# Attention iterations in another fixed order, with squares of q and k moved to POOL

## The chip, the cores and the metric

The kernel runs on one core of one Trainium2 chip. The core has five engines with a queue of instructions each: TensorE (PE: matmuls, and transposes that are done as matmuls with an identity), VectorE (DVE), ScalarE (ACT), GpSimd (POOL) and SyncE (SP), which issues most DMAs. An engine runs its queue in order; it waits for another engine through semaphores. Matmuls read SBUF and write PSUM; DVE and ACT read PSUM, POOL does not. The metric is the device time of one execution in microseconds (us).

## What is computed

Two encoder layers over 256 positions of 1024 features, in float32. Each layer has an attention half and an FFN half:

```python
h = rmsnorm(x, attn_norm[l])
c_q, c_kv, k_r, q_d, k_d, v_d = jnp.split(h @ w_in[l], split_at, axis=-1)
o_a = mla_mixer(c_q, c_kv, k_r, cos, sin, ...)          # 8 heads of 96, dense softmax over 256 keys
q_d = rmsnorm(q_d.reshape(B, S, DIL_HEADS, DIL_HD), g_dil_q[l])
k_d = rmsnorm(k_d.reshape(B, S, DIL_HEADS, DIL_HD), g_dil_k[l])
o_b = dilated_attention(q_d, k_d, v_d, rel_bias)        # 8 heads of 64, three patterns with bias
mixed = jnp.concatenate([o_a.reshape(B, S, -1), o_b.reshape(B, S, -1)], axis=-1)
x = x + mixed @ w_out[l]
x = x + conv_ffn(rmsnorm(x, ffn_norm[l]), w_up[l], conv_w[l], conv_b[l], w_down[l])
```

The norms of q_d and k_d need a sum of squares over the 64 features of each head. The three dilated patterns are folded into one additive matrix `Bn`, so a dilated head is a softmax over all 256 keys too.

## The kernel before

**Products in two parts.** Each float32 product is done as three faster matmuls: an operand is split into a high part and a low part, and hi x hi, lo x hi and hi x lo are summed in PSUM. The high part of a weight (`wh`) is a copy on ACT (L175), the low part (`wl`) is raw minus `wh` on DVE (L188); the same is done for activations (`xh` and `xl`, `mh` and `ml`). Weights stream in from DRAM by SP's DMAs, in units of 128x1024, and a ring of six units holds `wh` and `wl`. `W.fill()` splits the next unit when the ring has room; the low part lags by one unit, `LO_LAG`.

**One layer.** After the in-projections come nine iterations, n = 0 to 8. Iteration n computes the scores of head pair n (four MLA pairs, four dilated pairs, and nothing at n = 8), and finishes pair n - 1: it turns the probabilities p (transposes on PE, `turn_p`, L591), copies them from PSUM on ACT, multiplies by v (`values`, L600) and keeps the result as mh and ml (`keep_o`). `turn_qk` (L528) transposes q and k of the next pair into PSUM, and `keep_qk` copies k on ACT and q, with its gain, on DVE (L279). `maxima` and `normalise` run on DVE, `exponents` on ACT. The dilated maxima also add the bias (L566). The transposes of p, q and k use one PSUM buffer, tile name A: a new turn waits until the last one has been copied out. The scores use S, and the values O.

**Filling work.** In between, at `gemm()`, PE does steps from the list `steps`: what is left of the k projection, the v projection and the output projection (tile acc; six or three matmuls of 512 columns a step). `COUNTS` says how many steps an iteration takes, and they are spread evenly over four slots. The end of the output projection (`ou[5]`, `ou[6]` and `out_end`, which adds to x), the transposition and split of x (`xT_part`: turn on L431, gain on DVE, square and xh on ACT, xl on DVE) and the first blocks of the FFN (`up`, L1083 to L1085, with half of the input rows) follow.

**Dilated q and k.** `d_evac` copies a 128x512 tile of q or k from PSUM to `nat` on ACT, and squares it on ACT from PSUM; `d_sum` adds up the squares on DVE into `ssd`; `d_var` (POOL), one DVE round and a chain of small POOL operations make an inverse root (`rsqrt` in `d_factor`) for all heads, and `d_scale` multiplies the two `nat` tiles by it on POOL (L290). The dilated turns read these tiles.

**What sets the order.** The nine iterations stand in a `manual_schedule` for PE, DVE and ACT: the order of the code is the order of these queues. POOL's queue, and everything behind the iterations, is ordered by the scheduler.

Of the kernel before, what the change touches and what calls it, by code (L numbers as in the profile page):

```python
# [19 lines left out]
P = 128  # L20
# [27 lines left out]
START = 5  # L48
COUNTS = [3, 4, 4, 4, 4, 4, 5, 4, 3]
WARM = 8  # L50
# [86 lines left out]
class Weights:  # L137
# [60 lines left out]
    def fill(self, most=1):  # L198
        limit = min(len(self.units), self.n_done + W_BUFS - W_SLACK)
        for _ in range(most):  # L200
            if self.n_hi < limit:
                self.split_hi()
            if self.n_lo < self.n_hi - LO_LAG:
                self.split_lo()

    def get(self, u):
# [25 lines left out]
def encoder(ctx: ExitStack, tc: tile.TileContext, wpk, x, prm, cst, oh, rb, pos, out):  # L232
# [53 lines left out]
    def act(o, a, f, **kw):  # L286
        nc.scalar.activation(o, a, f, **kw)  # L287
# [220 lines left out]
    def run(steps):  # L508
        for s in steps:
            s()  # L510
# [100 lines left out]
    def layer(l, sx, late, bias):  # L611
# [26 lines left out]
        def d_evac(i, dst, t, a):  # L638
            act(dst[:, t, :], a, AF.Copy)
            sq = wide()  # L640
            act(sq, a, AF.Square)
            return sq
# [30 lines left out]
        def v_evac(t):  # L673
            act(vd[:, t, :], a_v[t], AF.Copy, scale=sx.r[:, t:t + 1])
# [241 lines left out]
        run(gk[:START - 3])  # L916
        hm = Heads(l, True, qm, km, vbox[0], pairs, fq)
        hm.turn_qk(0)
        hm.keep_qk(0)
# [53 lines left out]
        def iteration(n):  # L973
# [5 lines left out]
            turns = list(nxt[0].turns(nxt[1])) if nxt else []  # L979
            slots = 4 if nxt or cur else 2  # L980
            share = [len(todo) // slots + (i < len(todo) % slots) for i in range(slots)]

# [13 lines left out]
            def background():  # L996
                if side:
                    side.pop(0)()

            if n == 3:  # L1000
                v_evac(0)
                v_evac(1)
            if cur:
                cur[0].scores(cur[1])
                cur[0].maxima(cur[1])
            if prev:
                prev[0].turn_p(prev[1])
            if cur:
                cur[0].maxima(cur[1] + 1)
                cur[0].exponents(cur[1])  # L1010
            W.fill()
            gemm()
            if prev:
                prev[0].turn_p(prev[1] + 1)
            if cur:
                cur[0].exponents(cur[1] + 1)
            background()
            gemm()
            if prev:
                prev[0].values(prev[1])  # L1020
                prev[0].keep_o(prev[1])
            background()
            turn_next()
            if cur:
                cur[0].normalise(cur[1])
            W.fill()
            background()
            gemm()
            turn_next()
            if cur:  # L1030
                cur[0].normalise(cur[1] + 1)
            background()
            gemm()
            W.fill()
            while side:
                background()
            assert not todo

        with tc.manual_schedule(engines={mybir.EngineType.PE, mybir.EngineType.DVE, mybir.EngineType.Activation}):
            for n in range(HEADS + 1):  # L1040
                iteration(n)
        run(steps)
        run(ou[5][2:3])
        W.fill()

        def out_end(t, c):
            out_mm(7, t, c, final=True)
            xs = X[:, t, 512 * c:512 * c + 512]
            tt(xs, accs[t][c], xs, ALU.add)

        run(ou[5][3:])
        out_end(0, 0)
        out_end(1, 0)
        run(ou[6][2:])
        xT_part(sf, gf, 0, 0)
        xT_part(sf, gf, 1, 0)
        out_end(0, 1)
        out_end(1, 1)
        W.done(u_out[7])
        W.fill()  # L1060

# [75 lines left out]
        first = [[acc(), acc()], [bank(), bank()]]  # L1137
        for j in range(2):
            up(j, first[j], range(4))
            W.fill()  # L1140
        xT_part(sf, gf, 0, 1, tbank())
        xT_part(sf, gf, 1, 1, obank())
        for j in range(NF):
# [114 lines left out]
```

## Time and profile before

| | us |
|---|---|
| median of three runs | 660.03 (659.01 to 660.3) |
| the profiled execution | 659.02 |
| its span | 657.2 |
| PE busy | 636.5 (97%) |
| DVE busy | 493.7 (75%) |
| ACT busy | 399.6 (61%) |
| POOL busy | 67.5 (10%) |

The profiled execution took 1.8 us more than its span, and lies at the low end of the three runs. Busy shares are means over the whole execution; the places where PE waits are short, and are found in the lists of waits and in the timelines. A duration in a timeline is that of the instruction by itself; consecutive instructions of an engine overlap at their ends, so what an instruction costs in a row is the distance between starts.

### The profile page before, as it was taken

To read this page: it belongs to the slowest core of one execution; us is meant where nothing else is said; L and a number is where in the kernel's file an instruction comes from. 1 tells how busy PE (TensorE), PEld (TensorE's weight loads), DVE (VectorE), ACT (ScalarE), POOL (GpSimd) and SP (SyncE) were. 2 spreads that over 40 slices of the span, in tenths; PEclk is the share of its full clock that TensorE was granted. 3 is DMA by queue.
4 is the path that set the end of the run, shared out by engine and by line. 5 is a ranking of instruction groups with operands and counts; after the bars stand their busy time and mean duration, and the time that the engine had idled before them with its cause. 6 is when DMAs were issued, how large, how long until landed. Compare 5 with 4: busy or idle time off the path is not lost.

```text
span 657.2 us, 10655 instructions
## 1 busy us (share of the span) xinstructions
PE 636.5 (97%) x4018; PEld 554.3 (84%) x4018; DVE 493.7 (75%) x1006; ACT 399.6 (61%) x721; POOL 67.5 (10%) x177
## 2 busy tenths in 40 slices
PE   8989899989999999999999989999899999999997
PEld 7867676679999999999899876667899999999996
DVE  5796676677987777778699766667699777777773
ACT  6972976756755555555478467766385555555551
POOL 3850170000000000000001105400000000000000
PEclk9999999999999999999999999999899999999999
DMA  8759431252664555554347422313247545544401
GB/s 300 269 194 173 179 128 65 65 192 79 237 207 183 192 193 192 192 177 154 112 136 272 161 78 115 128 65 129 65 168 280 181 175 175 184 189 188 161 1 64
DMA packets 17708, 105.19 MB, mean 160 GB/s; under 512 B 2103, under 2 KB 3800, under 8 KB 6649
## 3 DMA queue, kind: packets, MB, share of 16 engines
q1 hardware_dynamic: 17656, 104.51, 45.9%
q8 instruction: 31, 0.51, 0.3%
q14 instruction: 21, 0.16, 0.1%
HBM read 103.20 MB, written 1.31 MB: 159 GB/s over the span
## 4 chain that ended last, share of the span: by engine, by line
PE 83%; POOL 6%; DVE 5%; ACT 2%; issue 2%; DMA 1%; SPq 1%; DVEq 0%; ACTq 0%; POOLq 0%
PE S L1085 12%; PE S L1084 12%; PE S L1083 12%; PE acc L1129 6%; PE acc L1128 6%; PE acc L1127 6%; PE acc L492 3%; PE acc L491 3%; PE acc L490 3%; PE O L600 3%; POOL s L295 3%; PE S L551 2%; PE A L591 2%; PE acc L935 2%; PE acc L938 2%; PE acc L937 2%
## 5 line engine op out<-in xcount | busy, mean ns | idle before, releaser
L175 ACT ACTIVATE wh<-raw 128x1024 fp32r<-128x1024 f32 (+3 forms) x188 | 193.2, 1036 | 110.6 <-PE S L1084 64.8
L188 DVE TENSOR_TENSOR wl<-raw,wh 128x1024 fp32r<-128x1024 f32 (+3 forms) x188 | 223.6, 1192 | 28.7 <-ACT wh L175 28.1
L1084 PE MATMUL S<-xl,wh 128*128 128x256 f32 x640 | 181.3, 284 | 0.0
L1085 PE MATMUL S<-xh,wl 128*128 128x256 f32 x640 | 180.9, 283 | 0.0
L1083 PE MATMUL S<-xh,wh 128*128 128x256 f32 x640 | 180.3, 283 | 0.0
L1084 PEld LDWEIGHTS S<-xl,wh 128*128 128x128 f32 x640 | 122.7, 192 | 1.5
L1083 PEld LDWEIGHTS S<-xh,wh 128*128 128x128 f32 x640 | 122.4, 192 | 1.6
L1085 PEld LDWEIGHTS S<-xh,wl 128*128 128x128 f32 x640 | 122.7, 192 | 0.1
L284 DVE SCALAR_TENSOR_TENSOR t<-t,prm_s,t 128x255 f32<-128x255 f32 x176 | 74.0, 480 | 1.0 <-ACT t L287 0.9
L1129 PE MATMUL acc<-wl,mh 128*128 128x512 f32 x176 | 69.3, 394 | 0.0
L1127 PE MATMUL acc<-wh,mh 128*128 128x512 f32 x176 | 69.3, 394 | 0.0
L1128 PE MATMUL acc<-wh,ml 128*128 128x512 f32 x176 | 69.2, 393 | 0.0
L490 PE MATMUL acc<-wh,xh 128*128 128x512 f32 (+2 forms) x160 | 61.3, 383 | 0.9 <-ACT nat L287 0.9
L492 PE MATMUL acc<-wl,xh 128*128 128x512 f32 (+2 forms) x160 | 58.2, 364 | 0.4 <-DVE wl L188 0.4
L491 PE MATMUL acc<-wh,xl 128*128 128x512 f32 (+2 forms) x160 | 57.8, 361 | 0.0
L287 ACT ACTIVATE t<-A 128x512 f32<-128x512 f32 (+2 forms) x56 | 28.1, 503 | 45.3 <-PE A L528 23.3
L287 ACT ACTIVATE t<-t,prm_s 128x256 f32<-128x256 f32 x88 | 47.9, 593 | 4.7 <-DVE t L275 4.7
L287 ACT ACTIVATE mh<-t 128x256 fp32r<-128x256 f32 x44 | 18.3, 416 | 47.7 <-DVE t L275 47.7
L275 DVE TENSOR_TENSOR t<-S,r2b 128x512 f32<-128x512 f32 (+1 forms) x42 | 28.0, 666 | 24.0 <-PE S L1085 24.0
L1129 PEld LDWEIGHTS acc<-wl,mh 128*128 128x128 f32 x176 | 33.1, 188 | 7.5
L1127 PEld LDWEIGHTS acc<-wh,mh 128*128 128x128 f32 x176 | 33.4, 190 | 5.9
L1128 PEld LDWEIGHTS acc<-wh,ml 128*128 128x128 f32 x176 | 33.1, 188 | 6.1
(168 smaller groups left out, 974.2 us busy)
## 6 DMA issues: line engine op xcount, KB each, us to landing
raw<-in_wpk_dram SPq DMA_DIRECT2D x86, 1024.0 KB, 4.8
raw<-in_wpk_dram SPq DMA_DIRECT2D x3, 896.0 KB, 4.6
raw<-in_wpk_dram SPq DMA_DIRECT2D x3, 768.0 KB, 4.9
raw<-in_wpk_dram SPq DMA_DIRECT2D x2, 816.0 KB, 5.9
Bn<-scr SPq DMA_DIRECT2D x8, 192.0 KB, 11.3
raw<-in_wpk_dram SPq DMA_DIRECT2D x2, 720.0 KB, 5.6
X<-in_x_dram SPq DMA_DIRECT2D x4, 256.0 KB, 5.3
raw<-in_wpk_dram SPq DMA_DIRECT2D x2, 384.0 KB, 5.6
```

Source lines behind the costliest of these rows:

```text
L175: self.nc.scalar.activation(hi[:, :n], self.raw[t][:, o:o + n], AF.Copy, scale=1.0 if g is None else g)
L188: self.nc.vector.tensor_tensor(out=lo[:, :n], in0=raw, in1=hi, op=ALU.subtract)
L287: nc.scalar.activation(o, a, f, **kw)
L490: mm(o, lhs.hi[:, k, sl], rh, start=k == 0, stop=False)
L491: mm(o, lhs.lo[:, k, sl], rh, start=False, stop=False)
L492: mm(o, lhs.hi[:, k, sl], rl, start=False, stop=k == ktot - 1)
L1083: mm(o, hi[:, kp], sf.hi[:, k, :], start=k == 0, stop=False)
L1084: mm(o, hi[:, kp], sf.lo[:, k, :], start=False, stop=False)
L1085: mm(o, lo[:, kp], sf.hi[:, k, :], start=False, stop=k == 7)
L1127: mm(o, m.hi[:, 0, sl], hi[:, cs], start=j == 0, stop=False)
L1128: mm(o, m.lo[:, 0, sl], hi[:, cs], start=False, stop=False)
L1129: mm(o, m.hi[:, 0, sl], lo[:, cs], start=False, stop=j == NF - 1)
```

## The change

Five things are changed.

- `COUNTS` and the new table `SHARES` give each iteration five slots for the filling steps, in place of four equal ones. The last iterations have 5 and 2 steps, where they had 4 and 3.
- The iteration is written in another order: both maxima first, a slot, `turn_p` of the first head, and `turn_next` ahead of the values. `W.fill` is divided into `fill_hi`, which stands twice in an iteration, and `fill_lo`, which stands two or three times and has no lag. `normalise` of the first head is ahead of the values, that of the second behind the first `fill_lo`. `v_evac` moves from the start of iteration 3 to the end of iteration 2.
- The manual order also covers the end of the output projection and the first two `up` blocks. `xT_part` is written out as `gained` (turn, gain, xh), `low` (xl) and `xT_square`, and the squares stand last.
- The squares of dilated q and k are computed on POOL from the copy in SBUF, four of 128x512 per layer.
- A one-column Exp stands ahead of the first `turn_qk`.

```diff
-COUNTS = [3, 4, 4, 4, 4, 4, 5, 4, 3]
+COUNTS = [3, 4, 4, 4, 4, 4, 5, 5, 2]
+SHARES = {(3, False, 2): (0, 0, 1, 1, 1), (4, True, 2): (0, 1, 1, 1, 1), (4, True, 1): (1, 1, 2, 0, 0),
+          (5, True, 1): (1, 1, 2, 1, 0), (5, True, 0): (1, 2, 2, 0, 0), (2, True, 0): (0, 1, 1, 0, 0)}
...
+    def fill_hi(self):
+        if self.n_hi < min(len(self.units), self.n_done + W_BUFS - W_SLACK):
+            self.split_hi()
+
+    def fill_lo(self):
+        if self.n_lo < self.n_hi:
+            self.split_lo()
...
             act(dst[:, t, :], a, AF.Copy)
             sq = wide()
-            act(sq, a, AF.Square)
+            ptt(sq, dst[:, t, :], dst[:, t, :], ALU.mult)
...
+        act(small(2)[:, :1], ones[:, :1], AF.Exp)
         hm.turn_qk(0)
...
-            slots = 4 if nxt or cur else 2
-            share = [len(todo) // slots + (i < len(todo) % slots) for i in range(slots)]
+            share = SHARES[len(todo), bool(prev), len(turns)]
+            share = list(share)
...
             if cur:
                 cur[0].scores(cur[1])
                 cur[0].maxima(cur[1])
+                cur[0].maxima(cur[1] + 1)
+            gemm()
+            if not side:
+                W.fill_lo()
+            background()
             if prev:
                 prev[0].turn_p(prev[1])
+            else:
+                turn_next()
             if cur:
-                cur[0].maxima(cur[1] + 1)
                 cur[0].exponents(cur[1])
-            W.fill()
             gemm()
             if prev:
                 prev[0].turn_p(prev[1] + 1)
             if cur:
                 cur[0].exponents(cur[1] + 1)
-            background()
             gemm()
+            if prev:
+                turn_next()
+            if cur:
+                cur[0].normalise(cur[1])
             if prev:
                 prev[0].values(prev[1])
                 prev[0].keep_o(prev[1])
-            background()
-            turn_next()
-            if cur:
-                cur[0].normalise(cur[1])
-            W.fill()
+            W.fill_hi()
+            W.fill_lo()
             background()
             gemm()
             turn_next()
             if cur:
                 cur[0].normalise(cur[1] + 1)
             background()
+            W.fill_hi()
+            background()
             gemm()
-            W.fill()
-            while side:
-                background()
+            W.fill_lo()
+            if n == 2:
+                v_evac(0)
+                v_evac(1)
...
+            out_end(0, 0)
+            out_end(1, 0)
+            run(ou[6][2:3])
+            pv0 = gained(0, 0, xT_turn(0, 0))
+            run(ou[6][3:])
+            pv1 = gained(1, 0, xT_turn(1, 0))
+            W.fill_hi()
+            low(0, 0, pv0)
+            low(1, 0, pv1)
+            W.fill_lo()
+            out_end(0, 1)
+            out_end(1, 1)
+            W.done(u_out[7])
+            xT_square(sf, 0, 0)
+            W.fill_hi()
+            W.fill_lo()
+            xT_square(sf, 1, 0)
```

Three places show what this does to the queues. The lines of the changed kernel have higher numbers for the same code (L290 becomes L300, L295 L305, L188 L190, L279 L289, L275 L285, L582 L592, L566 L576).

**POOL, layer 0, up to the start of the chain for dilated q.** `ssd` holds the sums of squares, `s` are small tiles of the chain, `nat_171` is q and `nat_172` is k. Before:

```order
L295 TENSOR_SCALAR s_739<-s_738 128x16 [waits Pool_49]
L295 TENSOR_SCALAR s_1053<-e_77_409 128x2 [waits DVE_49,Activation_49]
L295 TENSOR_SCALAR s_1052<-ssd_173,s_1053 128x8 [waits DVE_49,Pool_49]
L295 TENSOR_SCALAR s_1052<-ssd_173,s_1053 128x8 [waits DVE_49]
L290 TENSOR_TENSOR s_1061<-s_1058 128x16 [waits DVE_49]
L295 TENSOR_SCALAR s_1064<-s_1061 128x16 [waits Pool_49]
```

and in the changed kernel:

```order
L305 TENSOR_SCALAR s_739<-s_738 128x16 [waits Pool_49]
L300 TENSOR_TENSOR t_198_968<-nat_171 128x512 [waits Activation_49]
L300 TENSOR_TENSOR t_199_973<-nat_171 128x512 [waits Activation_49]
L305 TENSOR_SCALAR s_1064<-e_77_409 128x2 [waits DVE_49]
L305 TENSOR_SCALAR s_1063<-ssd_173,s_1064 128x8 [waits DVE_49,Pool_49]
L300 TENSOR_TENSOR t_245_1123<-nat_172 128x512 [waits Activation_49]
L305 TENSOR_SCALAR s_1063<-ssd_173,s_1064 128x8 [waits DVE_49]
L300 TENSOR_TENSOR s_1072<-s_1069 128x16 [waits DVE_49]
L305 TENSOR_SCALAR s_1075<-s_1072 128x16 [waits Pool_49]
L300 TENSOR_TENSOR s_1073<-s_1075,s_1063 128x16 [waits Pool_49]
L305 TENSOR_SCALAR s_1079<-s_1073 128x16 [waits Pool_49]
L300 TENSOR_TENSOR s_1078<-s_1079,s_1069 128x16 [waits Pool_49]
```

The two squares of q stand ahead of the chain, the first square of k stands between the two `d_var` of q; the second follows right behind the last row shown, inside the chain.

**DVE, layer 0, from the end of iteration 3 to the first dilated maxima.** The row L279 or L289 on A is `keep_qk`, the rows on t are `normalise`. Before:

```order
L275 TENSOR_TENSOR ml_1346<-O_1340,mh_1345 128x256 [waits Activation_49]
L279 TENSOR_SCALAR t_311_1354<-A_1349,gqk 128x256 [waits Activation_49]
L582 RECIPROCAL s_1358<-s_1302 128x2
L279 TENSOR_SCALAR t_291_1300<-t_291_1300,s_1358 128x256 [waits DVE_49]
L279 TENSOR_SCALAR t_291_1300<-t_291_1300,s_1358 128x256
L582 RECIPROCAL s_1365<-s_1315 128x2
L279 TENSOR_SCALAR t_297_1313<-t_297_1313,s_1365 128x256 [waits DVE_49]
L279 TENSOR_SCALAR t_297_1313<-t_297_1313,s_1365 128x256
L188 TENSOR_TENSOR wl_1374<-raw_923,wh_1288 128x1024
```

and in the changed kernel:

```order
L289 TENSOR_SCALAR t_309_1347<-A_1342,gqk 128x256 [waits Activation_49]
L592 RECIPROCAL s_1351<-s_1294 128x2
L289 TENSOR_SCALAR t_292_1292<-t_292_1292,s_1351 128x256 [waits DVE_49]
L289 TENSOR_SCALAR t_292_1292<-t_292_1292,s_1351 128x256
L285 TENSOR_TENSOR ml_1361<-O_1355,mh_1360 128x256 [waits Activation_49]
L190 TENSOR_TENSOR wl_1366<-raw_946,wh_1364 128x1024 [waits DMAHW2_49,Activation_49]
L592 RECIPROCAL s_1368<-s_1300 128x2
L289 TENSOR_SCALAR t_296_1298<-t_296_1298,s_1368 128x256 [waits DVE_49]
L289 TENSOR_SCALAR t_296_1298<-t_296_1298,s_1368 128x256
L190 TENSOR_TENSOR wl_1374<-raw_946,wh_1372 128x1024 [waits Activation_49]
L576 ISA t_318_1384,s_1385<-S_1378,Bn 128x256 [waits DMAHW5_49,DMAHW4_49,DMAHW6_49,DMAHW3_49,DMAHW7_49,DMAHW0_49,PE_49]
```

One weight split without a wait, ahead of the maxima, has become two, each waiting for ACT, with the second head's `normalise` between them. Iteration 4 ends in the same way, iterations 5 to 7 with one split.

**DVE, layer 0, iteration 8.** `t_377` and `t_382` (before), `t_378` and `t_381` (after) are p of the last two heads, which PE turns next. Before:

```order
L275 TENSOR_TENSOR ml_1657<-O_1651,mh_1656 128x256 [waits Activation_49]
L582 RECIPROCAL s_1660<-s_1619 128x2
L279 TENSOR_SCALAR t_377_1617<-t_377_1617,s_1660 128x256 [waits DVE_49]
L279 TENSOR_SCALAR t_377_1617<-t_377_1617,s_1660 128x256
L582 RECIPROCAL s_1667<-s_1631 128x2
L279 TENSOR_SCALAR t_382_1629<-t_382_1629,s_1667 128x256 [waits DVE_49]
L279 TENSOR_SCALAR t_382_1629<-t_382_1629,s_1667 128x256
L188 TENSOR_TENSOR wl_1676<-raw_1109,wh_1607 128x1024
```

and in the changed kernel:

```order
L592 RECIPROCAL s_1666<-s_1625 128x2 [waits Activation_49]
L289 TENSOR_SCALAR t_378_1623<-t_378_1623,s_1666 128x256 [waits DVE_49]
L289 TENSOR_SCALAR t_378_1623<-t_378_1623,s_1666 128x256
L285 TENSOR_TENSOR ml_1676<-O_1670,mh_1675 128x256 [waits Activation_49]
L190 TENSOR_TENSOR wl_1681<-raw_1313,wh_1679 128x1024 [waits DMAHW5_49,Activation_49]
L592 RECIPROCAL s_1683<-s_1630 128x2
L289 TENSOR_SCALAR t_381_1628<-t_381_1628,s_1683 128x256 [waits DVE_49]
L289 TENSOR_SCALAR t_381_1628<-t_381_1628,s_1683 128x256
```

The first head's `normalise` has moved ahead of ml, the second head's behind a weight split that waits for ACT.

## Rows read from the trace of the kernel before

**Rows 1.** The page: busy us, share and instructions of PE and PEld.

```profile
PE 636.5 (97%) x4018; PEld 554.3 (84%) x4018; DVE 493.7 (75%) x1006; ACT 399.6 (61%) x721; POOL 67.5 (10%) x177
```

**Rows 2.** A time window: busy us by engine, granted clock, DMA share, GB/s.

```profile
100.00:120.00 20.00, 20.00 (x112) 13.11 (x111) 14.04 (x51) 13.07 (x34) 0.00 (x0) 1.00 0.21 60
```

**Rows 3.** PE's waits, 62 to 165 us: total us, times, longest.

```profile
PE A L528 <- DVE t L279: 2.5, 3, 1.0
PE acc L1083 <- ACT xh L287: 2.1, 1, 2.1
PE S L551 <- DVE t L279: 0.7, 1, 0.7
```

**Rows 4.** The same view, 380 to 475 us (layer 1).

```profile
PE A L528 <- POOL nat L290: 0.2, 1, 0.2
```

**Rows 5.** Timeline of POOL: start, us, operation, idle before and releaser.

```profile
83.14 1.29 POOL L290 TENSOR_TENSOR s<-s,s 128x16 f32<-128x16 f32 x1
...
86.58 2.05 POOL L290 TENSOR_TENSOR nat<-nat,fd 128x512 f32<-128x512 f32 x2
...
90.30 0.28 POOL L295 TENSOR_SCALAR s<-ssd,e 128x8 f32<-128x8 f32 x1 [1.29 <-DVE ssd L645]
91.08 0.21 POOL L290 TENSOR_TENSOR s<-s 128x16 f32<-128x16 f32 x1 [0.50 <-DVE s L281]
...
97.73 2.04 POOL L290 TENSOR_TENSOR nat<-nat,fd 128x512 f32<-128x512 f32 x2
```

**Rows 6.** Timeline of PE, first dilated iteration.

```profile
101.48 1.13 PE L551 MATMUL S<-t,t 64*128 64x256 f32 x8
...
105.17 1.66 PE L600 MATMUL O<-t,nat 128*64 128x256 f32 x8
106.76 0.66 PE L528 MATMUL A<-cst_s,nat 128*128 128x128 f32 x4
107.17 0.47 PE L935 MATMUL acc<-wh,mh 128*128 128x512 f32 x1
...
108.73 1.14 PE L551 MATMUL S<-t,t 64*128 64x256 f32 x8
```

**Rows 7.** Timeline of DVE beside the stretched POOL operation.

```profile
83.12 1.22 DVE L188 TENSOR_TENSOR wl<-raw,wh 128x1024 fp32r<-128x1024 f32 x1
```

**Rows 8.** Timeline of DVE, first dilated iteration.

```profile
101.74 0.16 DVE L582 RECIPROCAL s<-s 128x2 f32<-128x2 f32 x1
...
102.46 1.22 DVE L188 TENSOR_TENSOR wl<-raw,wh 128x1024 fp32r<-128x1024 f32 x1
103.59 0.42 DVE L566 CUSTOM_DVE_ANT_0 t<-S,Bn 128x256 f32<-128x256 f32 x1
...
107.28 0.42 DVE L275 TENSOR_TENSOR ml<-O,mh 128x256 fp32r<-128x256 f32 x1 [2.23 <-ACT mh L287]
```

**Rows 9.** Timeline of ACT, the same stretch.

```profile
100.19 0.39 ACT L287 ACTIVATE t<-A 128x256 f32<-128x256 f32 x1 [0.56 <-PE A L528]
100.47 1.05 ACT L175 ACTIVATE wh<-raw 128x1024 fp32r<-128x1024 f32 x1
...
104.11 0.51 ACT L287 ACTIVATE t<-t,s 128x256 f32<-128x256 f32 x1 [0.28 <-DVE s L566]
...
105.12 0.57 ACT L287 ACTIVATE t<-A 128x512 f32<-128x512 f32 x1
...
106.86 0.39 ACT L287 ACTIVATE mh<-O 128x256 fp32r<-128x256 f32 x1 [0.18 <-PE O L600]
```

**Rows 10.** Timelines of DVE, ACT and PE at the first FFN matmul, layer 0.

```profile
141.42 0.69 DVE L275 TENSOR_TENSOR t<-S,prm_s 128x512 f32<-128x512 f32 x1
...
142.25 0.62 ACT L287 ACTIVATE xh<-t 128x512 fp32r<-128x512 f32 x1
...
142.92 0.50 PE L1083 MATMUL acc<-xh,wh 128*128 128x256 f32 x2 [2.06 <-ACT xh L287]
```

**Rows 11.** A time window in layer 1, columns as in rows 2.

```profile
462.90:466.30 3.40, 3.40 (x18) 3.40 (x17) 2.62 (x4) 1.25 (x3) 0.49 (x2) 0.51 0.40 169
```

More of the change, by code (lines that the diff above doesn't have):

```diff
@@ L1032, in iteration @@
             background()
+            W.fill_hi()
+            background()
             gemm()
[L1034 to L1036 removed]
+            W.fill_lo()
+            if n == 2:
+                v_evac(0)
+                v_evac(1)
+            assert not side
             assert not todo
@@ L1041, in layer, with out_end, gained, low @@
                 iteration(n)
[L1042 to L1060, printed above, removed]
+            run(steps)
+            run(ou[5][2:])
+            W.fill_hi()
+            W.fill_lo()
+            def out_end(t, c):
+                out_mm(7, t, c, final=True)
+                xs = X[:, t, 512 * c:512 * c + 512]
+                tt(xs, accs[t][c], xs, ALU.add)
+            def gained(t, c, pt):
+                tv = wide()
+                pv = tv.rearrange("p (k t) -> p k t", k=4)
+                tt(pv, pt.rearrange("p (k t) -> p k t", k=4),
+                   gf[:, 4 * c:4 * c + 4].unsqueeze(2).to_broadcast([P, 4, P]), ALU.mult)
+                act(sf.hi[:, 4 * c:4 * c + 4, t * P:t * P + P], pv, AF.Copy)
+                return pv
+            def low(t, c, pv):
+                sl = slice(t * P, t * P + P)
+                tt(sf.lo[:, 4 * c:4 * c + 4, sl], pv, sf.hi.bitcast(F32)[:, 4 * c:4 * c + 4, sl], ALU.subtract)
+            out_end(0, 0)
[12 more added lines that the diff above has]
+            xT_square(sf, 0, 0)
+            W.fill_hi()
+            W.fill_lo()
+            xT_square(sf, 1, 0)
         r2b = work.tile([P, SEQ], F32, name=nm("r2b"), tag="r2b", bufs=1)
@@ L1137, in layer @@
         first = [[acc(), acc()], [bank(), bank()]]
[L1138 to L1142, printed above, removed]
+        with tc.manual_schedule(engines={mybir.EngineType.PE, mybir.EngineType.DVE, mybir.EngineType.Activation}):
+            up(0, first[0], range(4))
+            W.fill_hi()
+            W.fill_lo()
+            pv2 = gained(0, 1, xT_turn(0, 1, tbank()))
+            up(1, first[1], range(4))
+            pv3 = gained(1, 1, xT_turn(1, 1, obank()))
+            low(0, 1, pv2)
+            low(1, 1, pv3)
+            xT_square(sf, 0, 1)
+            xT_square(sf, 1, 1)
         for j in range(NF):
```

3 lines of the change are left out of this document (removed).

## The prediction

> **What bounds the kernel now.** I read the page first: TensorE (PE) is busy 97% of the span [rows 1], so an edit can only pay where PE waits, or cost where it makes PE wait. The time windows say where it does not wait: between 100 and 120 us, in the dilated iterations, PE is busy 20.00 of 20 us [rows 2], so nothing is to be won there. The list of waits names the places that are left. In layer 0, PE waits 2.5 us in three pieces for DVE before turns of q and k (L528), 0.7 us for DVE before scores (L551), and 2.1 us for ACT's xh before the first FFN matmul (L1083) [rows 3]; each piece also costs about 0.16 us of a drained pipeline (the distance between the starts of the matmuls on both sides is that much more than the wait). That is 3.3 + 2.2 = 5.5 us, with drains near 6, in layer 0; layer 1 repeats it. One more row matters most: in layer 1 PE waits 0.2 us for POOL's scaled `nat` at L528 [rows 4]. The wait is small only because PE arrives late. The chain on POOL that scales k for the dilated heads ends at 97.73 + 2.04 = 99.77 us in layer 0 [rows 5], and PE turns that tile right behind it. So two chains run neck and neck up to the first dilated scores at 101.48 [rows 6], and removing PE's waits shortens one of them.
>
> **The change, part by part.** Sums are per layer, against the profiled execution: 659.0 us, of which 657.2 span. That run lies 1.0 below the median of the three.
>
> *First half (iterations 0 to 3).* Both maxima move ahead of the filling matmuls, the turns of q and k move earlier in DVE's and ACT's order, normalise comes earlier, and the dummy Exp loads the table while ACT waits for something else in the k chain. I followed each old wait of [rows 3] through the new order: the producer (keep_qk on DVE) no longer stands behind maxima or a weight split, and the three L528 pieces and the L551 piece vanish or shrink. That would bring PE to the turn of dilated pair 0 some 3.3 to 4 us earlier. But there it needs the POOL chain, and the change makes that longer. The square of k, t = 0, stands between the two `d_var` of q, and that of k, t = 1, inside the factor chain of q. A 128x512 operation on POOL takes 2.04 / 2 = 1.02 us [rows 5]. The q chain ended at 86.58 + 2.05 = 88.63; now at about 89.6 with one square inside, 90.6 if the other is late too. Then two `d_var` at about 0.3 each and the round over DVE, 90.30 to 91.08, then 91.08 to 99.77 [rows 5]: 89.6 + 0.3 + 0.3 + 0.5 + 8.7 = 99.4, against 99.77. Before, POOL stood idle ahead of 90.30 waiting for DVE's sum; that idle time is what pays for the square. The chain also holds two operations stretched to 1.29 us, 1.08 more than their neighbours, exactly while DVE splits a weight (83.14 against 83.12 [rows 5, 7]; four such pairs a layer). If both in the k chain fell elsewhere the chain would be 2.2 shorter; if both squares come late it is about 1.1 longer. Net: **-0.6 us** (-2.2 to +1.1), and PE now waits some 3 us in one piece where it waited in four.
>
> The Trainium skill (SBUF — State Buffer, section "SBUF: two separate sides") says that DVE and GpSimd hold a shared port pair exclusively for a whole instruction, when a DVE operation has two SBUF inputs and GpSimd reads SBUF; the other blocks. The trace agrees in one direction, the 1.29 beside the 1.22. By that rule a square would hold a weight split for up to 1.02 us, which no row shows; it is a rival below.
>
> *Dilated iterations 4 and 5.* Here the new order puts two weight splits on DVE at the tail of iterations 3 and 4 (before: one), each waiting for its copy on ACT, and those copies queue on ACT behind mh. Queued behind the second split are the maxima of the new scores; behind these, on ACT, the exponentials of the first head, and behind those the evacuation of the second turned p. PE's `turn_next` takes the same PSUM bank and waits for that evacuation. From rows, with T the start of scores: values end at T; mh starts 0.1 later (106.76, 106.86), the first copy 0.28 after mh (100.19, 100.47) and lasts 1.05 [rows 6, 9]: T + 1.45. The split then goes on to 1.13 later (102.46 to 103.59), normalise of the second head 0.72 (101.74 to 102.46) [rows 8], the second split 1.13: maxima start at T + 4.5. Before they started at 103.59, T + 2.1. The first exponential follows 0.52 after the first maximum (103.59, 104.11), two take 1.01, the evacuation 0.57 [rows 8, 9]: it ends at T + 6.6. PE reaches `turn_next` after scores, two turns and four steps: 3.69 (101.48 to 105.17) plus two steps, 1.56 (107.17 to 108.73) [rows 6]: T + 5.25. Wait 1.3. Iteration 5 starts from the same state, since keep, mh and the copies hang on PE's own progress: again 1.3. From iteration 6 there is one split, the evacuation ends at T + 5.5, and nothing is left. Sum **+2.6 us** (1.0 if one of the copies starts before mh, 3.2 with drains and late keep_qk).
>
> *Iteration 8.* Normalise of the last second head now stands behind the split of wl34, which waits for its copy, which waits for mh of the last pair but one. By the same rows: values end, + 0.38 for the copy's start, + 1.05, + 1.13, + 0.72: 3.35 us after the values. PE meanwhile has one turn of p (0.41) and one step (0.9), with about 0.25 in it for mh and ml (ml ends 0.84 after mh starts, rows 106.86 and 107.28 [rows 8, 9]): it is there at 1.6. Wait 1.75; before, no split stood between. **+1.8 us** (1.2 to 2.3).
>
> *Passage into the FFN.* Squares of x and the copies of weights now stand behind xh, and the last six output matmuls (1.4 us) lie behind the second turn. From the gain multiplication to xh 0.83, from xh to PE 0.67 (141.42, 142.25, 142.92 [rows 10]), with 0.4 for the turn's end 1.9, less 1.4 of cover: 0.5. The second matmul needs xl, 0.75 after xh, less 0.28: 0.45 more. So about 0.95 where 2.06 and its drain, 2.2, stood: **-1.3 us** (-0.5 to -2.2).
>
> *The rest at nothing.* The same matmuls run; ACT has four Squares less per layer, but PE doesn't wait for ACT there. `v_evac` is covered by the idle time before the k chain's end. The order by hand over the first two `up` blocks leaves later matmuls fed: the next xh is due 12 matmuls of 0.28 after its turn.
>
> *Clock.* After the 2.05-us wait in layer 1 the granted clock is 0.51 from 462.9 to 466.3 [rows 11], which is the lower level, 1.2 GHz: half of 3.4 us, 1.7, is lost. The same wait in layer 0 (2.06) has no such stretch. That loss goes with the wait, but new waits of about 3 us may bring it elsewhere. I take 0 (-1.7 to +5).
>
> **Sum.** -0.6 + 2.6 + 1.8 - 1.3 = +2.5 per layer, +5.0 in all: 659.0 + 5.0 = 664.0 for a run like the profiled one, 665.0 at the median. With all low ends 2 x (-2.2 + 1.0 + 1.2 - 2.2) - 1.7 = -6.1; the high ends alone give 2 x (1.1 + 3.2 + 2.3 - 0.5) = +12.2.
>
> **Rivals.**
> *The gains stand whole.* If the POOL chain ended some 4 us earlier than I think, and the splits found DVE free, each layer would give back 3.9 and 1.3, with the clock 12: 648. Against it: the 8.7 us of that chain are 20 small operations in a row. Chance 0.06.
> *Half the gain.* Stretches fall elsewhere and the new waits are at their low ends: 660.0 - 6.1 = 654. For it: in the row order DVE has slack before iteration 3. Chance 0.16.
> *No change.* One of the two new waits, that of iteration 8, is not there: 2 x (-0.6 + 2.6 - 1.3) = +1.4, less the clock's 1.7: 660. Or the passage gains all of 2.2. Chance 0.13.
> *Slower still, by the clock.* PE's 3-us wait for the POOL chain in each layer brings the lower level for 3.4 us afterwards, as at 462.9: 2 x 1.7 more, 668.5. It decides from about the length of the wait already seen to do it once in two cases. Chance 0.15.
> *Squares block splits.* Each of two squares a layer holds a split, and keep_qk behind it, by up to 1.02: 2 x 1.0 more, 667. Chance 0.08. The lock in the Trainium skill's rule would do this.
>
> **How the numbers follow.** The forecast, its own range 662 to 667, has 0.42. A measurement can tell about 0.2%, 1.3 us. Slower: 0.42 + 0.15 + 0.08 = 0.65; same 0.13; faster 0.22. The range leaves out the whole gain and the far upper end: 653.5 to 670.
>
> **What would show it.** Right: PE waits for POOL `nat` at L538 of about 3 us a layer; two waits of 1.3 for ACT's copy of A at L538 in the dilated iterations; one of 1.75 for DVE at L601 near their end; under 1.2 us before L1120. POOL shows 1-us squares between its small operations. Wrong: kd scaled before 97 us in layer 0, or first dilated scores before 99; dilated iterations still 7.25 us apart (101.48 to 108.73 [rows 6]); no wait at the last turn of p.

## The result, and the profile after

The changed kernel takes 668.58 us (median of 4 runs, 666.56 to 670.17) against 659.56 for the kernel before: a ratio of 1.0137, with a 95% interval of 1.0120 to 1.0153. It is slower by 9.0 us. Forecast were 665.0, 5.0 slower than the 660.0 known then; the result lies above the forecast's own range of 662 to 667 and inside the wide one of 653.5 to 670. The profiled execution took 668.44 us with a span of 666.7.

The page of the changed kernel, its busy line and its line of granted clock by slices; [rows 1] is the busy line before:

```profile
PE 640.5 (96%) x4018; PEld 557.1 (84%) x4018; DVE 499.5 (75%) x1006; ACT 393.2 (59%) x715; POOL 75.2 (11%) x185
...
PEclk8999998999999999999999999798999999999999
```

PE does the same 4018 matmuls, but is busy 4.0 us longer, and the granted clock is lower in three slices: the second 8 is a slice of layer 0's attention, the 7 and the last 8 are slices of layer 1's (the kernel before has a single 8, the stretch of [rows 11]; the first digit here is the start of the program).

Where the time is lost is seen by lining up the two traces at the same piece of work: the first score matmul of iterations 0, 4, 5, 6 and 7, and the steady FFN loop behind them (first matmul of its down projection). Distances in us, worked out from the timelines of PE:

| stretch | before, layer 0 | after | more | more, layer 1 |
|---|---|---|---|---|
| iteration 0 to 4 | 40.04 | 41.19 | +1.15 | +1.15 |
| iteration 4 to 5 | 7.25 | 8.42 | +1.17 | +1.28 |
| iteration 5 to 6 | 7.26 | 8.23 | +0.97 | +1.10 |
| iteration 6 to 7 | 7.26 | 7.82 | +0.56 | +0.57 |
| iteration 7 to the FFN loop | 44.48 | 45.18 | +0.70 | +0.62 |

With 0.2 us ahead of the first attention in layer 0, these are the whole +4.7 of each layer; through both FFN loops the two traces run in step, 4.73 and then 9.42 us apart.

The list of waits of PE, layer 0 (62 to 165 us; total, times, longest) stands against [rows 3]:

```profile
PE A L538 <- POOL nat L300: 2.6, 2, 2.1
PE S L561 <- DVE t L289: 1.6, 2, 0.9
PE A L601 <- DVE t L289: 1.6, 1, 1.6
PE A L538 <- ACT t L297: 1.4, 2, 1.2
PE O L1107 <- DVE t L289: 0.4, 1, 0.4
PE acc L1121 <- DVE xl L285: 0.3, 1, 0.3
```

The old waits at turns for DVE and the wait for xh are gone. In their place stand the POOL chain, the copy of A in a dilated iteration, the last turn of p, and, not foreseen, scores that wait for keep_qk (L561) twice in the place of once. The timeline of PE shows the pieces; the bracket is the idle time ahead:

```profile
80.56 0.70 PE L561 MATMUL S<-t,t 96*128 96x256 f32 x2 [0.88 <-DVE t L289]
...
99.50 0.48 PE L538 MATMUL A<-cst_s,nat 128*128 128x128 f32 x1 [2.06 <-POOL nat L300]
100.50 0.48 PE L538 MATMUL A<-cst_s,nat 128*128 128x128 f32 x1 [0.52 <-POOL nat L300]
...
117.69 0.66 PE L538 MATMUL A<-cst_s,nat 128*128 128x128 f32 x4 [1.20 <-ACT t L297]
...
137.22 0.50 PE L601 MATMUL A<-cst_s,t 128*128 128x128 f32 x2 [1.56 <-DVE t L289]
```

And the clock behind the first long wait, in windows (busy us by engine, granted clock, DMA share, GB/s):

```profile
98.00:102.00 4.00, 1.98 (x8) 1.08 (x10) 0.55 (x2) 0.38 (x1) 2.28 (x4) 0.69 0.63 250
102.00:106.00 4.00, 4.00 (x17) 2.22 (x14) 2.72 (x7) 2.27 (x3) 0.00 (x0) 0.50 0.00 0
106.00:110.00 4.00, 4.00 (x23) 2.78 (x21) 2.75 (x10) 2.77 (x9) 0.00 (x0) 0.96 0.35 109
```

From 102 to 106 us PE is busy all the time at 0.50, the lower level of 1.2 GHz. In finer windows the clock is 0.50 from 99.5 to 106.3: through the 3.3 us ahead of iteration 4, which begins at 102.81, and through the first 3.5 us of it. Iteration 4 shows no wait for the copy of A, which the forecast had put there; a PE at half speed arrives late enough.

### The profile page after: what moved, and what is told of

Its sections match the earlier page's. It is cut to its first block, busy times and chain, and to the rows that moved or that the text cites. A ratio compares the mean times of both kernels' runs of the same rounds, so it can differ in the third digit from the quotient of the medians.

```text
span 666.7 us, 10657 instructions
## 1 busy us (share of the span) xinstructions
PE 640.5 (96%) x4018; PEld 557.1 (84%) x4018; DVE 499.5 (75%) x1006; ACT 393.2 (59%) x715; POOL 75.2 (11%) x185
## 4 chain that ended last, share of the span: by engine, by line
PE 77%; DVE 9%; POOL 6%; ACT 3%; issue 2%; DMA 1%; SPq 1%; DVEq 0%; ACTq 0%
PE S L1120 11%; PE S L1122 11%; PE S L1121 11%; PE acc L1166 6%; PE acc L1165 6%; PE acc L1164 6%; PE acc L500 3%; PE acc L502 3%; PE acc L501 3%; DVE wl L190 3%; POOL s L305 3%; PE O L610 3%; PE S L561 2%; ACT t L297 2%; PE acc L946 2%
## 5 line engine op out<-in xcount | busy, mean ns | idle before, releaser
L190 DVE TENSOR_TENSOR wl<-raw,wh 128x1024 fp32r<-128x1024 f32 (+3 forms) x188 | 223.4, 1190 | 31.2 <-ACT wh L177 30.8
L285 DVE TENSOR_TENSOR t<-S,r2b 128x512 f32<-128x512 f32 (+1 forms) x42 | 27.9, 665 | 23.4 <-PE S L1122 23.4
L289 DVE TENSOR_SCALAR t<-A,gqk 96x256 f32<-96x256 f32 (+1 forms) x24 | 11.5, 481 | 37.6 <-ACT t L297 37.6
```

What stands on the lines that cost most here:

```text
L190: self.nc.vector.tensor_tensor(out=lo[:, :n], in0=raw, in1=hi, op=ALU.subtract)
```

## Experiments

Each timed run is compared with runs of the kernel before on the same chip (medians 659.2 to 660.2). Differences from the changed kernel are taken from its 668.58, which is of another series. A profile is one execution; the time up to the first scores alone differs between profiles (61.10 to 62.39 us in kernels that have the same code up to there), so edits are also weighed by the stretches of the table above.

**Squares back on ACT.** In the changed kernel, one line:

```diff
-            ptt(sq, dst[:, t, :], dst[:, t, :], ALU.mult)
+            act(sq, a, AF.Square)
```

> The changed kernel (668.6 us) with the squares of dilated q and k back on ACT. Theory 'DVE's order': in the changed kernel POOL sits idle 1.9 us ahead of the k chain, because DVE's sum of k's squares stands behind a weight split; so the chain ends where it did (PE's turn of dilated pair 0 still waits about 2.5 us for POOL) and the time stays within 1 us of 668.6. Rival 'the squares': the two squares among the chain's operations lengthen it by about 1 us each; the wait for nat falls to under 1.5 us, the stretch at the lower clock behind it goes, and the time falls by 2 to 6 us to 663 to 666.5.

663.95 us, ratio 1.0063 (1.0039 to 1.0087): the squares on POOL cost 4.6 of the 9 us. Neither theory foresaw where. The wait for nat is as long as it was, 2.7 us, but it begins and ends earlier. Waits of layer 0, and POOL ahead of the k chain and at its end:

```profile
PE A L538 <- POOL nat L300: 2.7, 2, 2.0
...
PE S L561 <- DVE t L289: 0.3, 1, 0.3
```

```profile
89.89 0.28 POOL L305 TENSOR_SCALAR s<-ssd,e 128x8 f32<-128x8 f32 x1 [2.10 <-DVE ssd L655]
...
97.20 2.04 POOL L300 TENSOR_TENSOR nat<-nat,fd 128x512 f32<-128x512 f32 x2
```

Counted from the first scores (62.36 here, 61.62 in the changed kernel), nat is ready at 36.9 against 38.8 us, and iteration 4 begins at 39.1 against 41.2 (39.2 in layer 1). The squares lengthen the way to it by 2 us a layer. The timelines show where: iteration 2 takes 11.85 us in the changed kernel and 10.28 here. Of these 1.6 us, the first square of k makes 1.2: it holds up the q chain's `d_var`, keep_qk is queued on DVE behind the step that waits for it, and the scores at 80.56 wait 0.88 us. The second square of k makes 0.4. In the changed kernel:

```profile
82.69 1.04 POOL L300 TENSOR_TENSOR t<-nat 128x512 f32<-128x512 f32 x1
```

```profile
83.00 0.75 DVE L294 SCALAR_TENSOR_TENSOR s<-s,fq 128x2 f32<-128x2 f32 x1
```

DVE's step between the maxima takes 0.16 us in this run and 0.75 beside the square; the exponentials follow later, and the turn at 85.59 waits 0.24 us for ACT. All that hangs on PE's iteration 2, DVE's sum for the k chain too, is later by as much. The same square also makes the q chain 0.9 us longer, but behind that POOL stands idle for 1.93 us anyway. That the squares cost the 2 us is shown by this run; the two shares are read from the timelines.

**Squares alone.** The kernel before, with the opposite edit.

> The kernel before (659.6 us) with only the squares moved to POOL. Theory 'DVE's order': POOL has 1.3 us of idle time ahead of the k chain, which takes one square; PE's wait for nat grows by at most 0.5 us a layer: 659.5 to 660.5. Rival 'the squares': the chain ends 1 to 2 us later, PE waits for nat by that much in each layer, 661.5 to 664.

662.78 us, ratio 1.0051 (1.0036 to 1.0067): the rival's time, but not its wait. PE waits for DVE and nowhere for nat. Here the scheduler put the squares elsewhere in POOL's queue, in layer 0 those of k behind the scaling of q, so the k chain starts at 93.79 (91.08 before, [rows 5]), and one turn of q and k in layer 0 waits 1.89 us for DVE, where keep_qk is queued behind a step of the chain that waits for POOL. Not all of the loss in the profile is the squares': in both layers the granted clock is at its lower level for 3.4 us in iteration 1 (0.50 from 392.9 to 396.3 in layer 1), and that iteration is 1.0 us longer than before. The trace shows one more cost. POOL, and DVE in the same microseconds:

```profile
70.39 2.81 POOL L290 TENSOR_TENSOR t<-nat 128x512 f32<-128x512 f32 x2 [20.52 <-ACT nat L287]
```

```profile
70.04 1.22 DVE L188 TENSOR_TENSOR wl<-raw,wh 128x1024 fp32r<-128x1024 f32 x1
...
71.76 1.59 DVE L279 TENSOR_SCALAR t<-t,s 128x256 f32<-128x256 f32 x2
```

Two such operations take 2.04 us elsewhere ([rows 5]); the first square waits for the weight split and both take 2.81. In return the normalise pair, which takes 0.62 us elsewhere, takes 1.59.

**The passage alone.** The kernel before, with the new order from the end of the output projection through the first two `up` blocks:

```diff
-        xT_part(sf, gf, 0, 0)
-        xT_part(sf, gf, 1, 0)
+            pv0 = gained(0, 0, xT_turn(0, 0))
+            run(ou[6][3:])
+            pv1 = gained(1, 0, xT_turn(1, 0))
...
+            low(0, 0, pv0)
+            low(1, 0, pv1)
...
+            xT_square(sf, 0, 0)
```

> The kernel before (659.6 us) with only the passage into the FFN in the new order (end of the output projection, split of x, first two up blocks); iterations, squares and table load as before. Theory: the wait for xh falls from 2.06 us to some 0.5 us in each layer, and with it goes the stretch at the lower clock in layer 1 (1.7 us): 2 x -1.0 - 1.7 gives 655.9, 655 to 657.5. Rival: the late squares of x hold up the statistics and the low part of x comes late, so that the gain is given back inside the FFN: 659 to 660.

657.07 us, ratio 0.9961 (0.9947 to 0.9975): faster than before, by 2.1 us, at the weak end of what was expected. The first matmul of the FFN on PE, against [rows 10]:

```profile
141.69 0.39 PE L1111 MATMUL acc<-xh,wh 128*128 128x256 f32 x1
142.42 0.39 PE L1112 MATMUL acc<-xl,wh 128*128 128x256 f32 x1 [0.34 <-DVE xl L283]
```

The wait of 2.06 has become one of 0.34 (with some 0.3 of drains). The rival is there in part: PE waits 0.4 us more for the statistics of x, whose squares now stand last on ACT, and from iteration 7 to the FFN loop layer 0 gains 0.6 us net (43.90 against 44.48). Layer 1 gains 2.2 there, since the old stretch at the lower clock is gone, but loses 1.0 in iteration 1, where no edit was made and PE had waited 0.95 us:

```profile
390.20:393.70 3.50, 3.44 (x10) 2.88 (x11) 3.40 (x10) 1.80 (x3) 0.28 (x1) 0.51 0.21 33
```

**PE kept busy during its wait.** In the changed kernel, ten matmuls into a PSUM buffer that the values overwrite; their result isn't used:

```diff
+            if n == 3:
+                busy = obank()
+                for _ in range(10):
+                    mm(busy, pairs[0].hi[:, 0, :P], W.get(W.n_done)[0][:, :512], start=True, stop=True)
             if prev:
                 turn_next()
```

> The changed kernel with ten extra 128x512 matmuls per layer (2.3 us, their result is not used) ahead of the first dilated turn, where PE waits 2.6 us for POOL; nothing else is changed, so the end of the POOL chain stays. Theory 'the idle PE loses its clock': with PE busy there is no stretch at 1.2 GHz behind the wait; the iteration that ran at half speed (about 3.2 us lost a layer) runs at full speed, but then meets the wait for ACT's copy that the slow iteration hid (1.2 to 1.4 us): 2 x -1.9 gives 664.8, 663.5 to 666. Rival 'the clock falls whatever PE does there': the stretch stays, 668 to 670.

666.29 us, ratio 1.0101 (1.0076 to 1.0127), 2.3 us less than the changed kernel: 0.3 above the range of the theory, and the four runs (665.2 to 667.8) overlap with those of the changed kernel. In the profile the clock did as the theory says; the same windows as above:

```profile
98.00:102.00 4.00, 3.37 (x20) 2.40 (x20) 0.00 (x0) 0.90 (x3) 2.84 (x6) 1.00 0.73 260
102.00:106.00 4.00, 3.89 (x26) 2.40 (x22) 3.49 (x10) 2.87 (x4) 0.00 (x0) 1.00 0.01 6
106.00:110.00 4.00, 2.79 (x16) 1.94 (x17) 2.44 (x9) 2.47 (x10) 0.00 (x0) 1.00 0.45 139
```

Granted clock 1.00 throughout, and between 106 and 110 PE is idle again: the wait for ACT's copy of A is back in iteration 4, as forecast for a PE at full speed. So of the half-speed stretch only 1.0 us a layer was a loss (iteration 0 to 4: 40.16 against 41.19); iteration 4 takes 8.37 us at full clock with the wait, and 8.42 with its first 3.5 us at half clock and without the wait. My expectation had this as 1.9 a layer. Without the ten matmuls, a stretch at the lower clock follows this wait in nine of ten layers (five profiles: the changed kernel, and those with the squares on ACT, the last normalise, the second split and the early sum); with them in none of two.

**The last normalise ahead of the split.** In the changed kernel:

```diff
             W.fill_hi()
-            W.fill_lo()
+            if n != HEADS - 1:
+                W.fill_lo()
...
                 cur[0].normalise(cur[1] + 1)
+            if n == HEADS - 1:
+                W.fill_lo()
```

> The changed kernel (668.6 us) with one weight split of iteration 7 (wl34) moved behind normalise of the second head, nothing else. Theory: PE's wait of 1.6 us before the last turn of p goes in both layers (1.7 with the drain), and in layer 1 the stretch at the lower clock that follows it (3.3 us at half speed, 1.7): 668.6 - 2 x 1.7 - 1.7 = 663.5, 662.5 to 665.5. Rival: the split is now late for its first use or the passage into the FFN takes the wait over: 667 to 669.

662.47 us, ratio 1.0047 (1.0034 to 1.0061): 6 us less, a little more than expected. The wait of 1.6 us is gone in both layers (0.2 us for ACT's copy is left), and the windows of layer 1's passage show the full clock. From iteration 7 to the FFN loop the profile is 1.4 us shorter in layer 0 and 2.9 in layer 1: 4.3 for the edit and the clock behind it. Another 1.7 fell in iterations 0 to 4, which the edit doesn't touch: there the stretch at the lower clock was 3.4 us long in place of 6.8. The small excess over the forecast is the clock's.

**The second split behind the maxima.** In the changed kernel:

```diff
             gemm()
-            W.fill_lo()
+            if n not in (3, 4):
+                W.fill_lo()
```

> The changed kernel (668.6 us) with the second weight split at the end of iterations 3 and 4 moved behind the next maxima, nothing else. Theory: the 1.2-us wait for ACT's copy of A in iteration 5 goes in both layers (1.4 with the drain); in iteration 4 nothing is gained, since PE at the lower clock comes late there anyway: 668.6 - 2.7 = 665.9, 665 to 667. Rival 'the wait moves': the split delays keep_qk or exponents in its new place and PE waits before the scores: 667.5 to 669.

662.75 us, ratio 1.0052 (1.0034 to 1.0070): 5.8 us less, twice what was expected. The wait for ACT's copy fell from 1.4 to 0.2 us a layer. In the profile, iteration 5 is shorter by 1.0 and 1.3 us in the two layers, as expected, and iteration 4 by 0.5 and 1.3, which the expectation had at nothing: at full clock it has no copy to wait for now. The remaining 1.8 us fell in iterations 0 to 4, ahead of the edit, and are the clock: the same waits for POOL (2.7 us in both layers) were followed by a stretch at the lower clock in layer 0 and by none in layer 1. The same 1.6-us wait at the last turn was followed by one in layer 0 and by none in layer 1, the other way round than in the changed kernel (+1.5 and -1.5 us). Two windows behind the wait for POOL, one in each layer:

```profile
102.00:106.00 4.00, 4.00 (x19) 2.86 (x18) 3.33 (x10) 2.46 (x4) 0.00 (x0) 0.65 0.00 0
...
426.00:430.00 4.00, 3.90 (x20) 2.69 (x19) 3.82 (x13) 3.10 (x8) 0.00 (x0) 1.00 0.01 4
```

The ten runs lie between 659.9 and 666.4, and they go with the clock: the granted clock, as a mean of the run, was 1.000 in the fastest, 0.989 and 0.987 in the two slowest (665.0 and 666.4), and 0.994 or 0.995 in the seven between (662.3 to 663.5). So between two such kernels some 2 us of a difference may be the clock and not the edit.

**DVE's sum of k's squares earlier.** In the changed kernel:

```diff
                 prev[0].keep_o(prev[1])
+            if n == 2:
+                background()
             W.fill_hi()
```

> The changed kernel (668.6 us), squares on POOL as in it, with only DVE's sum of k's squares ahead of the weight split in iteration 2. Theory: the k chain was late because that sum stood behind a split; POOL's idle time ahead of it (1.93 us) shrinks by some 1.1 us, PE's wait for nat falls from 2.6 to about 1.5 us, and the loss at the lower clock behind it becomes rarer: 663 to 666. Rival: keep_qk, which now stands behind the sum's round over POOL, holds PE before the scores by as much, and nothing is gained: 667.5 to 669.5.

666.80 us, ratio 1.0104 (1.0084 to 1.0124), 1.8 us less than the changed kernel: just short of the range expected. The chain did start 1.15 us earlier, but ended only 0.3 earlier. That is all the edit gives; the rest of the 1.8 us is in the profile the clock, whose stretch behind the wait was 3.4 us long in place of 6.8 and which stayed full in layer 1's passage. POOL in this run:

```profile
89.94 0.28 POOL L305 TENSOR_SCALAR s<-ssd,e 128x8 f32<-128x8 f32 x1 [0.80 <-DVE ssd L655]
90.72 1.11 POOL L300 TENSOR_TENSOR s<-s 128x16 f32<-128x16 f32 x1 [0.50 <-DVE s L291]
...
98.09 2.04 POOL L300 TENSOR_TENSOR nat<-nat,fd 128x512 f32<-128x512 f32 x2
```

and in the changed kernel:

```profile
88.88 0.28 POOL L305 TENSOR_SCALAR s<-ssd,e 128x8 f32<-128x8 f32 x1
91.09 0.28 POOL L305 TENSOR_SCALAR s<-ssd,e 128x8 f32<-128x8 f32 x1 [1.93 <-DVE ssd L655]
91.87 0.21 POOL L300 TENSOR_TENSOR s<-s 128x16 f32<-128x16 f32 x1 [0.50 <-DVE s L291]
...
98.40 2.04 POOL L300 TENSOR_TENSOR nat<-nat,fd 128x512 f32<-128x512 f32 x2
```

The first operation of the chain takes 1.11 us in place of 0.21: it now falls beside the split that the sum had been moved ahead of. Moved earlier, the chain of fifteen small POOL operations meets one split more.

**The four edits together.** Squares on ACT, the last normalise, the split behind the maxima and the early sum, in the changed kernel.

> The changed kernel with four edits: squares back on ACT (664.0 measured), the two moves of splits (last normalise, dilated maxima), and in iteration 2 DVE's sum of k's squares ahead of the weight split. Theory: the named waits account for the loss, so 664.0 - 2 x 1.7 - 2 x 1.3 - 2 x 1.1 = 655.8, 653.5 to 657.5, below the kernel before (659.2). Rival: the POOL chain still ends late enough that PE loses its clock behind the wait: 658 to 661.

653.82 us, ratio 0.9910 (0.9887 to 0.9934): 14.8 us less than the changed kernel, and 5.5 below the kernel before. The list of waits of layer 0 has one large row left:

```profile
PE A L538 <- POOL nat L300: 2.4, 2, 1.8
PE O L1113 <- DVE t L289: 0.4, 1, 0.4
PE S L561 <- DVE t L289: 0.3, 1, 0.3
PE acc L1127 <- DVE xl L285: 0.3, 1, 0.3
PE A L601 <- ACT t L297: 0.3, 1, 0.3
```

The sum of the named waits gave 655.8. In this profile no stretch at the lower clock follows the wait that is left, in either layer; that was no term of the sum and is worth 1.0 us a layer by the run with the busy PE.

**The kernel before with the passage and the table load.** To the passage alone one line is added:

```diff
+        act(small(2)[:, :1], ones[:, :1], AF.Exp)
         hm.turn_qk(0)
```

> The kernel before with the new passage into the FFN (657.1 measured) and the one-column Exp ahead of the first turn, which moves the table load of 1.28 us off the way to the first exponentials. Theory: the first wait at L528 (0.96 us in each layer) goes with it: 657.1 - 2 x 1.0 = 655.1, 654 to 656.3. Rival: what PE gains there it waits for the POOL chain of k later, which ends when it did: 656.5 to 657.5.

654.05 us, ratio 0.9912 (0.9893 to 0.9932): 3.0 us less than the passage alone. The early Exp removes one of three waits at the turns of q and k, and iterations 0 to 4 are 1.3 us shorter than in the kernel before in both layers. The POOL chain doesn't take the gain back, because its inputs come earlier too: the k chain's sum is taken up at 89.00 in place of 90.30, and nat is ready at 98.46 in place of 99.77, with the first scores at 61.44 in both. In the profiles another 1.0 us is the stretch at the lower clock that the passage alone had in layer 1 and this run hasn't.

**The same with earlier squares of x.** Two squares ahead of the last xh:

```diff
+            xT_square(sf, 0, 1)
+            xT_square(sf, 1, 1)
             pv3 = gained(1, 1, xT_turn(1, 1, obank()))
             low(0, 1, pv2)
             low(1, 1, pv3)
-            xT_square(sf, 0, 1)
-            xT_square(sf, 1, 1)
```

> The kernel before with the new passage and the early table load (654.05 us), and the same two squares of x ahead of the last xh. Theory: the wait of 0.4 us for the statistics of x (0.55 with the drain) goes in both layers: 653.0, 652.5 to 653.6. Rival: xh is later by the squares and the first full up block waits for it: 654 to 655.5.

653.25 us, ratio 0.9903 (0.9884 to 0.9921), as expected; the wait for the statistics is no longer in the list, and the last stretch is 0.6 us shorter in each layer of the profile. The step of 0.8 us between the medians is about the size of the spread between runs.

**The mended kernel with work put into the wait.** To the four edits come the two squares of x, and two filling steps moved from iterations 6 and 7 to iteration 3, ahead of the turn that waits for POOL:

```diff
-COUNTS = [3, 4, 4, 4, 4, 4, 5, 5, 2]
+COUNTS = [3, 4, 4, 6, 4, 4, 4, 4, 2]
...
-          (5, True, 1): (1, 1, 2, 1, 0), (5, True, 0): (1, 2, 2, 0, 0), (2, True, 0): (0, 1, 1, 0, 0)}
+          (6, True, 1): (1, 1, 4, 0, 0), (4, True, 0): (1, 2, 1, 0, 0), (2, True, 0): (0, 1, 1, 0, 0)}
```

> The mended kernel (653.8 us) with two of the filling steps of iterations 6 and 7 moved to iteration 3, ahead of the first dilated turn, where PE still waits 2.4 us for POOL, and with two squares of x (t = 0 and 1, second half) ahead of the last xh. Theory: the wait for nat falls by the two steps, 1.4 us, and the wait of 0.4 us in the first FFN statistics goes: 2 x -1.8 gives 650.2, 649.5 to 652. Rival: the steps are missed in iterations 6 and 7, where PE then waits for DVE and ACT: 652.5 to 654.5.

650.51 us, ratio 0.9862 (0.9846 to 0.9878): the fastest of all, 9.6 us below the kernel before on its chip (660.15). Two things were changed at once here, and their shares were not run apart. The waits of layer 0:

```profile
PE A L538 <- POOL nat L300: 1.0, 2, 0.7
PE S L561 <- DVE t L289: 0.4, 1, 0.4
PE acc L1127 <- DVE xl L285: 0.3, 1, 0.3
PE A L601 <- ACT t L297: 0.3, 1, 0.3
```

The run before this one has the same passage, table load and squares of x in the old order of iterations, and takes 653.25. So the new order of iterations, with its waits removed, is worth 2.7 us; as first written it lost more than that to what stood queued ahead of short, urgent work.

## Why the prediction was right, and what it had wrong

**The two new waits** were right in place and size. The maxima of iteration 5 start 4.3 us behind its scores (T + 4.5 in the prediction), after two splits. DVE from the first split on, and the score matmul they belong to:

```profile
111.23 1.14 PE L561 MATMUL S<-t,t 64*128 64x256 f32 x8
```

```profile
112.55 1.22 DVE L190 TENSOR_TENSOR wl<-raw,wh 128x1024 fp32r<-128x1024 f32 x1 [0.31 <-ACT wh L177]
...
114.41 1.22 DVE L190 TENSOR_TENSOR wl<-raw,wh 128x1024 fp32r<-128x1024 f32 x1
115.55 0.42 DVE L576 CUSTOM_DVE_ANT_0 t<-S,Bn 128x256 f32<-128x256 f32 x1
```

PE waits 1.20 us (1.3 predicted) at 117.69. The other wait, in iteration 4, is hidden by the lower clock in the changed kernel and is there, 1.21 us, in the run with the busy PE. Over iterations 4 to 6 the stretches sum to +2.7 us in layer 0 and +2.95 in layer 1, against +2.6. Part of the agreement is luck: iteration 4 lost its 1.2 us to the clock and not to the copy, and iteration 6, where "nothing is left" was predicted, lost 0.56. It has five filling steps where iterations 4 and 5 have four. In the kernel before, the fifth step cost nothing (7.26 us with five, 7.25 with four); in the new order it costs itself: 7.82 with five, and 7.10 in the same iteration with four, in the run with work put into the wait. That the split in iteration 5 costs this much is shown by the run that moved it.

**The last turn of p** waited 1.56 us (1.75 predicted). Moving one split removes it and brings 1.4 us in layer 0 (1.8 predicted), since PE then waits 0.2 for ACT.

**The passage** has the right wait and half the gain. The last stretch is +0.7 us in layer 0, where the prediction had 1.8 - 1.3 = +0.5, but as +1.4 for the last turn and -0.7 for the passage: two terms that were too large cancel. By itself the passage gives -0.6. The wait for xh did go. What took the gain back is the 0.4 us wait (0.55 with the drain) for the statistics in the FFN, which was not in the sum: with the squares of x earlier, the same passage gives -1.15. "The next xh is due 12 matmuls of 0.28 after its turn" was true, in that no such wait is in the list, but the squares behind it have a reader as well.

**The first half** is the term that was mis-sized: -0.6 predicted, +1.15 measured in both layers. That makes 3.5 of the 4.4 us between the 664.0 forecast and the 668.44 of the profile. Two steps of it failed.

First, the clock was set to 0, with the loss a layer put among the rivals. PE's wait of 2.6 us was followed by the lower clock in both layers of the profile, and the run with the busy PE shows its price, 1.0 us. The old stretch in layer 1, which the forecast let go with the wait for xh, came back behind the last turn of p (0.50 from 461.3 to 464.7). The rival "slower still, by the clock" was nearest to the result, 668.5 against 668.58, and that nearness is luck: the low clock's price was 1.0 and not 1.7 a layer, and the rest is made up by the second step.

Second, the chain on POOL ended 0.5 us later than before, counted from the first scores (38.8 against 38.3), where the sum said 0.4 earlier. "Before, POOL stood idle ahead of 90.30 waiting for DVE's sum; that idle time is what pays for the square" does not hold: the idle time is still there, and longer, 1.93 us, because DVE gets to that sum later. DVE, in the order of its queue:

```profile
87.50 1.42 DVE L289 TENSOR_SCALAR t<-t,s 128x256 f32<-128x256 f32 x2
88.85 0.41 DVE L285 TENSOR_TENSOR ml<-O,mh 128x256 fp32r<-128x256 f32 x1
89.18 1.21 DVE L190 TENSOR_TENSOR wl<-raw,wh 128x1024 fp32r<-128x1024 f32 x1
90.31 0.67 DVE L655 TENSOR_REDUCE ssd<-t 128x8 f32<-128x512 f32 x1
```

The sum (last row) stands behind a split of 1.2 us that used to be elsewhere, and behind a normalise that takes 1.42 us in place of 0.62, beside POOL's scaling of q (86.68 to 88.78). But these alone don't make the chain late: with the squares on ACT the same split and a normalise of 1.32 stand there, and the chain ends 1.4 us earlier than in the kernel before (36.9 against 38.3). What made it late is the 1.6 us that the squares cost PE and DVE in iteration 2. The prediction followed POOL's queue with care, charged the squares as time on POOL, and followed DVE's queue only up to keep_qk.

Three small slips change nothing: the waits of [rows 3] sum to 3.2 and 2.1, not to 3.3 and 2.2; 665.0 and 2 x 1.7 make 668.4; and the k chain has 15 small operations, not 20.

**Squares that block DVE** was a rival with the right edit and mostly another mechanism. It had a square hold a weight split; the larger part was the order of POOL's queue, and in the iterations no split takes more than 1.23 us. But POOL's square does hold shorter operations of DVE, beside the 0.75 for 0.16 above also a normalise. In the changed kernel:

```profile
68.33 1.04 POOL L300 TENSOR_TENSOR t<-nat 128x512 f32<-128x512 f32 x1 [18.87 <-ACT nat L297]
```

```profile
68.38 1.40 DVE L289 TENSOR_SCALAR t<-t,s 128x256 f32<-128x256 f32 x2
```

The Trainium skill (SBUF — State Buffer, section "SBUF: two separate sides") says that the loser of the shared port pair blocks for the whole instruction; the 1.40, and the 1.59 beside the squares alone, agree with that. The chance of 0.08 was too small: squares on POOL cost 4.6 us in the new order and 3.6 in the old, by several ways at once, the clock among them, of which the runs don't give each its share.

## What to carry to other kernels

When an edit shortens the way of one engine to a meeting point, find the second chain that ends there and walk every queue it passes, also the engine that hands it one number in the middle. Put long operations that are needed late (weight splits) behind short ones that are needed soon (normalise, maxima, sums), because an in-order queue makes everyone behind wait for their producers too. Fill an unavoidable wait of PE with real work: it wins the time of the work, and in both layers of the run with ten matmuls in the wait the clock stayed full.

## What the runs showed of the hardware

POOL and DVE hold each other up in both directions. POOL's operations of 0.2 us take 1.1 to 1.3 beside a weight split (1.22); DVE's normalise pair of 0.62 takes 1.42 beside a 128x512 multiplication on POOL, and 1.40 and 1.59 beside squares. The reduction for the maxima, which DVE reads from PSUM, kept its 0.68 us beside a square (70.83 in the changed kernel).

Whether a stretch at the lower clock follows isn't told by the length of one wait. One wait of 2.06 us in the kernel before had none behind it in layer 0, and its like of 2.05 had one in layer 1. A wait of 0.95 us was followed by one in layer 1 of the run with the passage alone, and the same wait in layer 0 by none. Waits for POOL of 2.6 to 2.7 us were followed by a stretch at 0.5 in both layers of the changed kernel and in one of two layers of the run with the split behind the maxima (0.65 and 1.00 in the windows shown); those of 2.4 us in both layers of the run with the early sum and in no layer of the kernel with the four edits. What decides it stays open.
